# Encoder block on one core: row-maximum scores in 64-row matmuls, two key blocks at a time, with 1024-column maxima

## The chip, the core and the metric

One Trainium2 chip, one of its cores. The metric is the time of one execution of the whole program on the device, in microseconds (us); lower is better. The engines are TensorE (PE in the profile, its weight loads shown apart as PEld), VectorE (DVE), ScalarE (ACT), GpSimd (POOL) and SyncE (SP), which here only issues transfers.

## What is computed

One layer of a bidirectional encoder in float32 with 2048 tokens, width 1024, 8 query heads of 64 columns that share 2 key/value heads, four pooling groups and a gated MLP of width 2816. Cut to what the change touches:

```python
h = rmsnorm(x, norm1_g[l]) * (1.0 + sc1) + sh1
proj = h @ w_in[l]                       # q | k | v | pool channels
q = apply_axial_rope(rmsnorm(q, q_norm_g[l]), tables)
k = apply_axial_rope(rmsnorm(k, k_norm_g[l]), tables)
s = jnp.einsum('bqkgd,bskd->bkgqs', qblk, k).astype(jnp.float32)   # q already times 1/8
p = jax.nn.softmax(s, axis=-1)
o = jnp.einsum('bkgqs,bskd->bqkgd', p, v)
mix = jnp.concatenate([att, pool], axis=-1) @ w_out[l]
x = x + g1 * mix                          # then the gated MLP, also added to x
```

## The kernel before

The program has three stages. The first projects the tokens into q, k, v and pool channels and writes q and k, transposed, to scratch in DRAM. The second is attention with the output projection. The third is the gated MLP. Only the second is touched, but for one copy in the first that lays k out for it.

Every float32 value that goes through TensorE is kept as two parts of a faster type, a high part (hi) and the rest (lo). A q tile `qa` has hi in partitions 0 to 63 and lo in 64 to 127; a key tile `kA` has hi in both halves. One matmul over 128 rows therefore gives (q_hi + q_lo) k_hi. A second matmul over 65 rows adds q_hi k_lo and, with a row of ones in `kB` at partition 64, minus the row maximum, which stands in partition 64 of `qb`.

Attention runs over 32 units, each one head and 512 queries (`gen_unit`). A unit goes over 16 key tiles of 128 keys. For each: two matmuls into `S` (L731, L732), two exponentials on ScalarE (L735 into `ph`, L736 in place), one subtraction on VectorE (L737 into `pl`), a running sum on GpSimd (L741) and two matmuls with v (L723 into `A`, L724 into `B`).

The row maxima of unit u+1 are worked out while unit u runs (`gen_max`, called as `nxt`): for each of four query tiles and four blocks of 512 keys, one matmul over 128 rows into one of two PSUM banks `pmx` (L692) and one VectorE reduction over 512 columns into `mx` (L694). Then `nm` is the negated maximum (L697), four small matmuls turn it into a row (L701), and ScalarE copies the row into `qb` (L702). Unit 0 has 12 of its 16 blocks done in the first stage.

A third stream, the filler, spreads the output projection of earlier chunks (L820, with L842 on VectorE) and the second norm's transposes (L860) over the units. The last chunk's output projection starts in PSUM banks that attention leaves (`gen_tail_pool`).

The order on each engine is set by a scheduler from the order of writing and the buffers; each engine then runs its instructions in that order and waits on semaphores. Loads of q go through the queue of SP from unit 3 on, of the first units through that of POOL.

Of the kernel before, what the change touches and what calls it, by code (L numbers as in the profile page):

```python
# [18 lines left out]
P = 128  # L19
# [4 lines left out]
HD = 64  # L24
# [23 lines left out]
class InOrder:  # L48
    """An engine whose instructions stay in the order in which they are written."""

# [14 lines left out]
def hybrid_block(ctx: ExitStack, tc: tile.TileContext, x, c, w_ada, b_ada, norm1_g, w_in,  # L65
# [14 lines left out]

# [1 line left out]
    q_scr = tc.dram_tile([NH, P, T], F32, name="q_scr")  # L82
# [9 lines left out]

# [1 line left out]
    const = ctx.enter_context(tc.tile_pool(name="const", bufs=1))  # L94
# [28 lines left out]

    # =============== mixer input projection ===============
    with tc.tile_pool(name="p1", bufs=1) as p1, \
            tc.tile_pool(name="ps1", bufs=1, space=PSUM) as ps1:
        # columns of w_in: q, k, v first (their space is free first), then u
        wi_hi, wi_lo = ([p1.tile([P, KD, n], F32R, name=f"wi_{nm}{n}") for n in (768, 512)]
# [171 lines left out]

        # scale and shift of the first norm; the first tokens' norm beside them
        h0 = gen_h(0)
# [16 lines left out]

        # weights, split, in the order of use  # L320
        bufs_w = [stage(), stage(), small("qst", [P, NH, P], F32), small("qhl", [P, NH, 2, HD]),
# [17 lines left out]

        # 1/count at the clipped edges  # L340
        edge = p1.tile([P, NG, 16], F32, name="edge")
# [68 lines left out]
        def gen_rope(b, tok, raw, cs_t, res):  # L410
# [25 lines left out]
            for i in range(2):  # L436
                S.copy(out=khl[:, :, i], in_=raw[:, 8:10])
            V.tensor_tensor(out=khl[:, :, 2], in0=raw[:, 8:10], in1=khl[:, :, 0].bitcast(F32),
                            op=ALU.subtract)
            S.copy(out=khl[:, :, 3], in_=ones.rearrange("p (a d) -> p a d", a=2))  # L440
            yield
# [7 lines left out]
        def gen_tr(tok, qhl, khl):  # L449
            """q as (hi, lo), k as (hi, hi) and (lo, one), transposed"""  # L450
            for _ in range(4):
                yield
            tr = ps1.tile([P, 4, P], F32R, tag="tr", name=f"trk{tok}", bufs=1)
            for a in range(NKV):
                for i in range(2):
                    PE.transpose(out=tr[:, 2 * i + a],
                                 in_=khl[:, a, 2 * i:2 * i + 2].rearrange("p a d -> p (a d)"),
                                 identity=identr)
                    yield
            kst = p1.tile([P, 2 * NKV, P], F32, tag="kst", name=f"kst{tok}", bufs=1)  # L460
            S.copy(out=kst, in_=tr.bitcast(F32))
            SP.dma_start(out=k_scr[:, :, :, tok:tok + P].rearrange("i a p t -> p (i a) t"), in_=kst)
            if tok >= T - BT:
                qst = stage().rearrange("p (h t) -> p h t", t=P)
            else:
                qst = p1.tile([P, NH, P], F32, tag="qst", name=f"qst{tok}", bufs=1)
            for hb in range(2):
                tr = ps1.tile([P, 4, P], F32R, tag="tr", name=f"tr{tok}_{hb}", bufs=1)
                for h in range(4):
                    PE.transpose(out=tr[:, h], in_=qhl[:, hb * 4 + h].rearrange("p a d -> p (a d)"),  # L470
                                 identity=identr)
                    yield
                S.copy(out=qst[:, hb * 4:hb * 4 + 4], in_=tr.bitcast(F32))
            SP.dma_start(out=q_scr[:, :, tok:tok + P].rearrange("h p t -> p h t"), in_=qst)

        def windows(b, us, res):
            """column i is token t0 - 8 + i, at column 8 + i of u; the last block has 8 more"""
            last = b == NB - 1
# [73 lines left out]
        def gen_early_max():  # L552
            """the row maxima of the first unit over the keys of the blocks that are done"""
            k0 = p1.tile([P, KD, BT], F32R, tag="h_hi", name="k_early", bufs=2).rearrange("p k t -> p (k t)")
# [73 lines left out]

    # =============== attention and output projection ===============
    ctx3 = ctx.enter_context(ExitStack())  # L630
    with tc.tile_pool(name="po", bufs=1, side="right", reuse_waits="tile") as po, \
# [7 lines left out]
        kB = p2.tile([P, NKV, T], F32R, name="kB")  # L639
        # per key tile: [v_lo 0 | v_hi 0 | ones | v_hi 1 | v_lo 1]  # L640
        vt = p2.tile([P, NKT, 5 * HD], F32R, name="vt")
# [13 lines left out]
        def load_kv(a, parts=((0, T - BT), (T - BT, T))):  # L655
            for t0, t1 in parts:
                for i, (m, n) in enumerate(((kA, P), (kB, 65))):
                    ld(a, m[0:n, a, t0:t1], k_scr[i, a, 0:n, t0:t1])
                ld(a, vt[:, t0 // P:t1 // P, 192 * a:192 * a + P],
                   v_scr[t0:t1, a].rearrange("(n p) d -> p n d", p=P))  # L660
# [9 lines left out]
        NU = len(units)  # L670
        qtiles = {}

        def load_q(u):
# [6 lines left out]
            (G if u < QG else QE).dma_start(out=qa.bitcast(F32), in_=q_scr[h, :, cs])  # L680
            (G if u < QG else QE).dma_start(out=qb[0:64].bitcast(F32), in_=q_scr[h, 0:64, cs])
            qtiles[u] = (qa, qb)

        def gen_max(u):
            c_, h = units[u]
            a = h // 4
            qa, qb = qtiles[u]
            mx = p2.tile([P, 4, 4], F32, tag="mx", name=f"mx{u}", bufs=2) if u else mx0
            for jq in range(0 if u else 4 * JP, 16):
                for j, qt in ((jq // 4, jq % 4) if u == 0 else (jq % 4, jq // 4),):  # L690
                    ps = ps2.tile([P, 512], F32, tag="mx", name=f"pmx{u}_{qt}_{j}", bufs=2)
                    PE.matmul(ps, qa[:, qt * P:(qt + 1) * P], kA[:, a, j * 512:(j + 1) * 512],  # L692
                              start=True, stop=True)
                    V.tensor_reduce(out=mx[:, qt, j:j + 1], in_=ps, axis=AX.X, op=ALU.max)  # L694
                    yield
            nm = p2.tile([P, 4], F32R, tag="nm", name=f"nm{u}", bufs=2)
            V.tensor_reduce(out=nm, in_=mx, axis=AX.X, op=ALU.max, negate=True)  # L697
            row = ps2.tile([P, 512], F32, tag="mx", name=f"row{u}", bufs=2)
            yield
            for qt in range(4):  # L700
                PE.matmul(row[0:1, qt * P:(qt + 1) * P], nm[:, qt:qt + 1], identr, start=True, stop=True)  # L701
            S.copy(out=qb[64:65, :], in_=row[0:1, :])  # L702
            yield
# [7 lines left out]
        def gen_unit(u):  # L711
# [16 lines left out]
            for kt in range(NKT):  # L728
                ks = slice(kt * P, (kt + 1) * P)
                s = ps2.tile([P, 512], F32, tag="S", name=f"S{u}_{kt}", bufs=3)  # L730
                PE.matmul(s, kA[:, a, ks], qa, start=True, stop=False)  # L731
                PE.matmul(s, kB[0:65, a, ks], qb[0:65], start=False, stop=True)  # L732
                ph = p2.tile([P, QC], F32R, tag="ph", name=f"ph{u}_{kt}", bufs=4)
# [92 lines left out]
        def gen_out(c_, half, wait=0):  # L826
            """x1 = x + pool half, then x1 += attention half."""
            if half == 1:
# [16 lines left out]
        def gen_ln2(t, x1, junk, hts, bank, stat, wait):  # L845
            """normalised x1, transposed"""
            tok = t * P
# [29 lines left out]
        LW = (4, 4)  # L877
        # the last chunk's output projection: the pool half first, in banks that the attention leaves
        tails = []

        def gen_tail_pool(tags, mix):
            for tag, bufs in tags:
                t, n = divmod(len(tails), 2)
                ps = ps2.tile([P, 512], F32, tag=tag, name=f"pt{t}_{n}", bufs=bufs)
                tails.append(ps)
                yield from gen_half(ps, mix, 1, t, n, True, False)

        mix3 = []

        def gen_first():  # L890
            mix3.extend(load_mix(NC - 1))
            for _ in range(12):
                yield
            yield from gen_tail_pool((("misc", 1), ("mx", 2), ("mx", 2)), mix3)

# [49 lines left out]

        # =============== gated conv MLP: Winograd's form of Strassen's product ===============
        pa = ctx3.enter_context(tc.tile_pool(name="pa", bufs=1, reuse_waits="tile"))
# [11 lines left out]
        def gen_ops(p, res):  # L959
            """the moving operands of part p, split"""  # L960
            o0, no, N = PARTS[p]
# [53 lines left out]
        def gen_w(p, j, res):  # L1015
            """the stationary operands of one pair of column tiles, split, in the order of use"""
            raw = []
# [82 lines left out]
    with tc.tile_pool(name="p3", bufs=1, reuse_waits="tile") as p3, \  # L1100
# [5 lines left out]
        def gen_wd(p, j, n, tag=""):  # L1106
            """w_down times the gate, split: worked out with the first part, kept in DRAM for the others"""
            rs, ns = slice(j * P, (j + 1) * P), slice(n * 512, (n + 1) * 512)
# [83 lines left out]
        def gen_gate(p, j, ug, uv):  # L1192
            """the depthwise convolution, the gate and its split"""
            o0, no, N = PARTS[p]
# [45 lines left out]
        def residual(p, i):  # L1240
            """half a tile of x1, to be added to the sum so far"""
            t, n = divmod(i, 2)
# [168 lines left out]
```

## Time and profile before

| | us |
|---|---|
| median of 3 runs | 2740.19 |
| lowest and highest run | 2736.31, 2745.56 |
| span of the profiled execution, first to last instruction | 2741.8 |
| of it, attention, from the first row maximum to the last unit | 380 to 1240 |
| TensorE, VectorE, ScalarE, GpSimd busy over the span | 2594.1, 2370.5, 1475.5, 1767.0 |

The page gives busy time as the union of the records of an engine. Matmul records overlap, since each is longer than the distance to the next one; so TensorE is better read from the starts of its matmuls than from its busy share.

### The profile page before, as it was taken

What the parts mean: (1) busy time and instruction counts of PE and PEld (TensorE: products, weight loads), DVE (VectorE), ACT (ScalarE), POOL (GpSimd) and SP (SyncE); (2) the same over time, 40 slices, a digit from 0 to 9 for tenths busy, and PEclk for the clock granted to TensorE, in tenths of its full rate; (3) what the DMA queues carried; (4) which work ended last, traced back from release to release, by engine and by line L of the source; (5) the groups of instructions that cost most, each with busy time, mean ns of one, the idle gap of its engine ahead of it and who ended that gap; (6) DMA issues with size and microseconds to landing.
All of it is one profiled execution on the core that took longest, in us unless ns stands there. A gap on an engine that the chain in (4) does not pass through costs nothing.

```text
span 2741.8 us, 39488 instructions
## 1 busy us (share of the span) xinstructions
PE 2594.1 (95%) x13439; PEld 2242.1 (82%) x13439; DVE 2370.5 (86%) x3526; ACT 1475.5 (54%) x2656; POOL 1767.0 (64%) x1397
## 2 busy tenths in 40 slices
PE   5899989999999999999899999899999998999999
PEld 5788867777776767767888888789999997999998
DVE  7778688989999998887999999978888888898886
ACT  5566457777778777775533443543333334533342
POOL 1222146556657666565888888697777776988883
PEclk9899989999999999999999999999999999999999
DMA  9685374331221222225444444443333224433332
GB/s 291 232 258 179 99 239 149 106 95 60 64 80 55 71 72 76 80 64 179 151 130 133 128 130 123 145 132 105 100 104 100 93 87 132 147 123 120 106 110 93
DMA packets 318164, 338.65 MB, mean 124 GB/s; under 512 B 24655, under 2 KB 226329, under 8 KB 317961
## 3 DMA queue, kind: packets, MB, share of 16 engines
q1 hardware_dynamic: 316953, 332.31, 38.4%
q0 software_dynamic: 1008, 3.81, 0.5%
q8 instruction: 106, 1.74, 0.3%
q14 instruction: 97, 0.79, 0.1%
HBM read 249.42 MB, written 86.63 MB: 123 GB/s over the span
## 4 chain that ended last, share of the span: by engine, by line
PE 36%; DVE 13%; issue 3%; ACT 1%; POOL 1%; POOLq 0%; DVEq 0%; ACTq 0%
PE pp L1156 23%; PE py L1233 13%; DVE y L1238 3%; DVE ac L1202 2%; DVE ac L1205 2%; DVE b L993 1%; DVE t L993 1%; ACT ac L1199 1%; PE pl L1354 1%; DVE wds L56 0%; DVE wdl L1123 0%; DVE ac L1212 0%; DVE ug L1176 0%; DVE uv L1171 0%; DVE uv L1174 0%
## 5 line engine op out<-in xcount | busy, mean ns | idle before, releaser
L1035 POOL TENSOR_TENSOR wl_s<-s,wh_s 128x512 fp32r<-128x512 f32 x260 | 390.3, 1502 | 187.8 <-ACT wh_s L1033 186.6
L1238 DVE TENSOR_TENSOR y<-py,y 128x512 f32<-128x512 f32 x620 | 418.5, 682 | 95.5 <-PE py L1233 94.8
L741 POOL TENSOR_TENSOR acc<-acc,ph 128x512 f32<-128x512 f32 x352 | 463.4, 1316 | 41.0 <-ACT ph L735 15.7
L1156 PE MATMUL pp<-t,wh_s 128*128 128x322 f32 (+1 forms) x1584 | 390.2, 322 | 7.0 <-DVE x L1072 3.2
L737 DVE TENSOR_TENSOR pl<-S,ph 128x512 fp32r<-128x512 f32 x512 | 348.7, 684 | 38.5 <-ACT S L736 31.5
L735 ACT ACTIVATE ph<-S 128x512 fp32r<-128x512 f32 x512 | 307.3, 600 | 131.9 <-PE S L732 116.2
L694 DVE TENSOR_REDUCE mx<-pmx 128x1 f32<-128x512 f32 x500 | 338.1, 681 | 27.0 <-PE pmx L692 25.2
L1035 POOL TENSOR_TENSOR wl_a<-wr,wh_a 128x512 fp32r<-128x512 f32 x195 | 312.9, 1605 | 22.7 <-ACT wh_a L1033 22.6
L1233 PE MATMUL py<-wdh,gh 128*128 128x512 f32 x674 | 275.7, 409 | 47.1 <-DVE y L1238 40.6
L736 ACT ACTIVATE S<-S 128x512 f32<-128x512 f32 x512 | 306.4, 598 | 0.0
L1156 PEld LDWEIGHTS pp<-t,wh_s 128*128 128x128 f32 x1584 | 282.2, 190 | 27.8 <-DVE t L993 4.1
L1033 ACT CAST wh_s<-s 128x512 fp32r<-128x512 f32 x264 | 161.9, 617 | 226.8 <-PE pp L1156 197.0
L1156 PE MATMUL pp<-b,wh_a 128*128 128x322 f32 (+1 forms) x1056 | 267.9, 323 | 1.3 <-DVE b L993 0.8
L1233 PE MATMUL py<-wdh,gl 128*128 128x512 f32 x674 | 268.8, 399 | 0.0
L1233 PE MATMUL py<-wdl,gh 128*128 128x512 f32 x674 | 268.8, 399 | 0.0
L1156 PE MATMUL pp<-t,wl_s 128*128 128x322 f32 (+1 forms) x792 | 254.3, 321 | 0.0
L724 PE MATMUL B<-pl,vt 128*128 128x512 f32 x512 | 210.5, 411 | 6.2 <-DVE pl L737 6.0
L1033 ACT CAST wh_a<-wr 128x512 fp32r<-128x512 f32 x198 | 122.3, 618 | 165.6 <-PE pp L1156 158.4
L723 PE MATMUL A<-ph,vt 128*128 128x512 f32 x512 | 204.7, 408 | 5.2 <-ACT ph L735 5.2
L692 PE MATMUL pmx<-kA,qa 128*128 128x512 f32 x500 | 203.3, 408 | 3.9 <-DMA kA<-k_scr 3.0
L739 POOL TENSOR_TENSOR acc<-ph,ph 128x512 f32<-128x512 f32 x32 | 41.3, 1290 | 256.8 <-ACT ph L735 226.9
L732 PE MATMUL S<-qb,kB 65*128 65x512 f32 x512 | 202.8, 402 | 1.1 <-ACT qb L702 0.8
(273 smaller groups left out, 6784.4 us busy)
## 6 DMA issues: line engine op xcount, KB each, us to landing
wr<-in_w_up_dram SPq DMA_DIRECT2D x132, 512.0 KB
wdh<-wd_scr SPq DMA_DIRECT2D x88, 256.0 KB
wdl<-wd_scr SPq DMA_DIRECT2D x88, 256.0 KB
stage<-in_w_ada_dram SPq DMA_DIRECT2D x36, 512.0 KB
x_scr<-x SPq DMA_DIRECT2D x48, 256.0 KB
wds<-in_w_down_dram SPq DMA_DIRECT2D x44, 256.0 KB
wd_scr<-wdh SPq DMA_DIRECT2D x44, 256.0 KB
wd_scr<-wdl SPq DMA_DIRECT2D x44, 256.0 KB
```

Of the source, the lines that this page charges most:

```text
L694: V.tensor_reduce(out=mx[:, qt, j:j + 1], in_=ps, axis=AX.X, op=ALU.max)
L723: PE.matmul(A, vt[:, kt, 192 * a:192 * a + P], ph, start=kt == 0, stop=kt == NKT - 1)
L724: PE.matmul(B, vt[:, kt, 64 + 64 * a:192 + 64 * a], pl, start=kt == 0, stop=False)
L735: S.activation(out=ph, in_=s, func=AF.Exp, scale=0.125)
L736: S.activation(out=s, in_=s, func=AF.Exp, scale=0.125)
L737: V.tensor_tensor(out=pl, in0=s, in1=ph.bitcast(F32), op=ALU.subtract)
L741: G.tensor_tensor(out=acc, in0=acc, in1=ph.bitcast(F32), op=ALU.add)
L1033: S.copy(out=hf, in_=src)
L1035: eng.tensor_tensor(out=lf, in0=src, in1=hf.bitcast(F32), op=ALU.subtract)
L1156: mm = PE.matmul(ps, l_[:, k], r_[:, k, 0:N], start=k == 0 and m == 0, stop=k == 3 and m == 2)
L1233: PE.matmul(ps, l_[:, ts_], r_, start=i == 0, stop=i == 3 * len(js) - 1)
L1238: V.tensor_tensor(out=ys[t][:, ns], in0=ps, in1=ys[t][:, ns], op=ALU.add)
```

## The change

Each maximum is now taken over q_hi k_hi alone. A pair of key blocks is scored by two matmuls over 64 rows, one on partitions 0 to 63 (`qa`, key block 2jj) and one on partitions 64 to 127 (`qb`, key block 2jj+1), into the two banks of one PSUM tile. One VectorE reduction then takes the maximum over 1024 columns. To have q_hi in both places, `qb` is loaded twice, and the row of minus maxima moves to its partition 0; `kB` therefore has (one and zeros) in its upper half and lo in its lower, and the second matmul of `S` goes over 128 rows. The buffer ring of two single banks becomes one tile of two banks.

```diff
-            V.tensor_tensor(out=khl[:, :, 2], in0=raw[:, 8:10], in1=khl[:, :, 0].bitcast(F32),
+            V.tensor_tensor(out=khl[:, :, 3], in0=raw[:, 8:10], in1=khl[:, :, 0].bitcast(F32),
                             op=ALU.subtract)
-            S.copy(out=khl[:, :, 3], in_=ones.rearrange("p (a d) -> p a d", a=2))
+            S.copy(out=khl[:, :, 2], in_=onesz[:, 127:191].unsqueeze(1).broadcast_to([P, NKV, HD]))
...
-                for i, (m, n) in enumerate(((kA, P), (kB, 65))):
-                    ld(a, m[0:n, a, t0:t1], k_scr[i, a, 0:n, t0:t1])
+                for i, m in enumerate((kA, kB)):
+                    ld(a, m[:, a, t0:t1], k_scr[i, a, :, t0:t1])
...
-            (G if u < QG else QE).dma_start(out=qb[0:64].bitcast(F32), in_=q_scr[h, 0:64, cs])
+            for r in (0, 64):
+                (G if u < QG else QE).dma_start(out=qb[r:r + 64].bitcast(F32), in_=q_scr[h, 0:64, cs])
...
-            mx = p2.tile([P, 4, 4], F32, tag="mx", name=f"mx{u}", bufs=2) if u else mx0
-            for jq in range(0 if u else 4 * JP, 16):
-                for j, qt in ((jq // 4, jq % 4) if u == 0 else (jq % 4, jq // 4),):
-                    ps = ps2.tile([P, 512], F32, tag="mx", name=f"pmx{u}_{qt}_{j}", bufs=2)
-                    PE.matmul(ps, qa[:, qt * P:(qt + 1) * P], kA[:, a, j * 512:(j + 1) * 512],
-                              start=True, stop=True)
-                    V.tensor_reduce(out=mx[:, qt, j:j + 1], in_=ps, axis=AX.X, op=ALU.max)
-                    yield
+            def pair(nm):
+                return ps2.tile([P, 2, 512], F32, tag="mx", name=f"{nm}{u}", bufs=1)
...
+                mx = p2.tile([P, 4, 2], F32, tag="mx", name=f"mx{u}", bufs=2)
+                for qt in range(4):
+                    qs = slice(qt * P, (qt + 1) * P)
+                    for jj in range(2):
+                        ps = pair(f"pmx{qt}_{jj}_")
+                        for t, q_ in ((0, qa), (1, qb)):
+                            r, j = slice(64 * t, 64 * t + 64), 2 * jj + t
+                            PE.matmul(ps[:, t], q_[r, qs], kA[r, a, j * 512:(j + 1) * 512],
+                                      start=True, stop=True)
+                        yield
+                        V.tensor_reduce(out=mx[:, qt, jj:jj + 1], in_=ps.rearrange("p a n -> p (a n)"),
+                                        axis=AX.X, op=ALU.max)
+                        yield
...
-            row = ps2.tile([P, 512], F32, tag="mx", name=f"row{u}", bufs=2)
+            row = pair("row")[:, 0]
...
-            S.copy(out=qb[64:65, :], in_=row[0:1, :])
+            S.copy(out=qb[0:1, :], in_=row[0:1, :])
+            maxed.append(u)
...
-                PE.matmul(s, kB[0:65, a, ks], qb[0:65], start=False, stop=True)
+                PE.matmul(s, kB[:, a, ks], qb, start=False, stop=True)
```

Unit 0 keeps single 512-column maxima, and the tail's pool half takes both banks of the pair at once, after the last maxima are done.

On TensorE, in the third unit (its score tiles are `S`, the row maxima of the fourth unit are `pmx`), before:

```order
L731 MATMUL S_4_4928<-qa_4259,kA 128x512
L732 MATMUL S_4_4928<-qb_4260,kB 128x512
L723 MATMUL A_4858<-ph_2_4895,vt 128x512
L724 MATMUL B_4859<-pl_2_4896,vt 128x512
L692 MATMUL pmx_1_0_4939<-kA,qa_4538 128x512
L731 MATMUL S_5_4944<-qa_4259,kA 128x512
L732 MATMUL S_5_4944<-qb_4260,kB 128x512
L723 MATMUL A_4858<-ph_3_4910,vt 128x512
L724 MATMUL B_4859<-pl_3_4911,vt 128x512
L692 MATMUL pmx_1_1_4955<-kA,qa_4538 128x512
```

and at the same key tiles now:

```order
L754 MATMUL S_4_4896<-qa_4261,kA 128x512
L755 MATMUL S_4_4896<-qb_4262,kB 128x512
L746 MATMUL A_4829<-ph_2_4865,vt 128x512
L747 MATMUL B_4830<-pl_2_4866,vt 128x512
L754 MATMUL S_5_4912<-qa_4261,kA 128x512
L755 MATMUL S_5_4912<-qb_4262,kB 128x512
L712 MATMUL pmx_0_3_4907<-kA,qa_4523 128x512
L712 MATMUL pmx_0_3_4907<-kA,qb_4524 128x512
L746 MATMUL A_4829<-ph_3_4880,vt 128x512
L747 MATMUL B_4830<-pl_3_4881,vt 128x512
```

A single `pmx` matmul per key tile has become two neighbours per two key tiles. There are 248 such pairs; in 237 the two stand next to each other, in 11 one full matmul stands between them. From the end of one pair to the start of the next there are mostly 7 to 13 other matmuls.

On VectorE, at the same place, before:

```order
L737 TENSOR_TENSOR pl_4_4932<-S_4_4928,ph_4_4931 128x512
L694 TENSOR_REDUCE mx_4868<-pmx_1_0_4939 128x1
L737 TENSOR_TENSOR pl_5_4948<-S_5_4944,ph_5_4947 128x512
L694 TENSOR_REDUCE mx_4868<-pmx_1_1_4955 128x1
L694 TENSOR_REDUCE mx_4868<-pmx_1_2_4970 128x1
L737 TENSOR_TENSOR pl_6_4963<-S_6_4959,ph_6_4962 128x512
```

and now:

```order
L760 TENSOR_TENSOR pl_4_4900<-S_4_4896,ph_4_4899 128x512
L760 TENSOR_TENSOR pl_5_4916<-S_5_4912,ph_5_4915 128x512
L715 TENSOR_REDUCE mx_4839<-pmx_0_3_4907 128x1
L760 TENSOR_TENSOR pl_6_4929<-S_6_4925,ph_6_4928 128x512
L715 TENSOR_REDUCE mx_4839<-pmx_1_3_4936 128x1
```

Sixteen reductions per unit have become eight of twice the columns, each between one or two subtractions.

## Rows read from the trace of the kernel before

**Rows 1.** The page: the span, and each engine's busy us (share of it) xinstructions.

```profile
span 2741.8 us, 39488 instructions
...
PE 2594.1 (95%) x13439; PEld 2242.1 (82%) x13439; DVE 2370.5 (86%) x3526; ACT 1475.5 (54%) x2656; POOL 1767.0 (64%) x1397
```

**Rows 2.** Windows over attention: length, then each engine's busy us (instructions), granted clock, DMA.

```profile
380.00:600.00 220.00, 212.84 (x895) 163.70 (x895) 192.36 (x316) 155.55 (x287) 128.65 (x99) 0.97 0.45 146
600.00:800.00 200.00, 198.37 (x855) 153.68 (x854) 182.04 (x300) 147.46 (x275) 121.47 (x94) 1.00 0.21 65
800.00:1240.00 440.00, 421.60 (x1797) 312.47 (x1796) 396.84 (x646) 345.96 (x654) 282.03 (x234) 0.99 0.25 73
```

**Rows 3.** The same windows, matmuls of L692 (the row-maximum scores) alone.

```profile
380.00:600.00 220.00, 54.45 (x130) 25.66 (x130) 0.97 0.45 146
600.00:800.00 200.00, 47.55 (x120) 22.61 (x120) 1.00 0.21 65
800.00:1240.00 440.00, 101.25 (x251) 47.60 (x250) 0.99 0.25 73
```

**Rows 4.** Groups on VectorE, 600 to 800 us: busy us, mean ns | idle before, releaser.

```profile
L694 DVE TENSOR_REDUCE mx<-pmx 128x1 f32<-128x512 f32 x119 | 80.7, 681 | 5.1 <-PE pmx L692 4.7
...
L697 DVE TENSOR_REDUCE nm<-mx 128x4 fp32r<-128x16 f32 x8 | 1.3, 164 | 0.0
```

**Rows 5.** Line L860: ns min/median/max, first and last start, form.

```profile
L860 PE MATMUL tp<-ident,lx x96: 270/272/421, 806.1 to 1186.2; 128*128 128x128 f32 x96
```

**Rows 6.** Timeline of PE in attention: start us, length us, line, tiles, rows*columns of the array.

```profile
702.53 0.40 PE L732 MATMUL S<-qb,kB 65*128 65x512 f32 x1
...
704.86 0.40 PE L692 MATMUL pmx<-kA,qa 128*128 128x512 f32 x1
```

**Rows 7.** Timeline of DVE over the same stretch.

```profile
701.37 0.67 DVE L694 TENSOR_REDUCE mx<-pmx 128x1 f32<-128x512 f32 x1
...
702.57 0.67 DVE L694 TENSOR_REDUCE mx<-pmx 128x1 f32<-128x512 f32 x1
```

**Rows 8.** Waits from 600 to 800 us: total us, times, longest us.

```profile
PEld B L724 <- DVE pl L737: 4.1, 10, 1.1
...
PEld pmx L692 <- DVE mx L694: 0.8, 3, 0.3
```

**Rows 9.** Timeline of PE where full-height matmuls alternate with one-row ones.

```profile
236.10 1.12 PE L242 MATMUL mr<-macc,ones 128*128 128x512 f32 x2 [0.78 <-DVE macc L200]
237.16 1.12 PE L243 MATMUL mr<-stage,ones 1*128 1x512 f32 x2
...
240.31 0.39 PE L374 MATMUL pu<-h_hi,wi_hi 128*128 128x256 f32 x1
240.54 0.28 PE L374 MATMUL pu<-h_lo,wi_hi 128*128 128x256 f32 x1
240.66 0.29 PE L374 MATMUL pu<-h_hi,wi_lo 128*128 128x256 f32 x1
```

**Rows 10.** The same place, a narrower window: the second matmul of the first block alone.

```profile
236.63 0.59 PE L242 MATMUL mr<-macc,ones 128*128 128x512 f32 x1
```

**Rows 11.** The same place, a weight load (PEld) after the last one-row block.

```profile
240.31 0.19 PEld L374 LDWEIGHTS pu<-h_hi,wi_hi 128*128 128x128 f32 x1 [0.76 <-DVE win L490]
```

**Rows 12.** Timeline of PE around the one-column matmuls of a unit's end.

```profile
893.34 0.40 PE L758 MATMUL B<-al,onesr 128*128 128x512 f32 x1
893.57 0.40 PE L701 MATMUL row<-identr,nm 128*1 128x128 f32 x4
893.81 0.45 PE L692 MATMUL pmx<-kA,qa 128*128 128x512 f32 x1
894.10 0.64 PE L820 MATMUL po<-wo,atth 128*128 128x512 f32 x2
```

**Rows 13.** VectorE on 1024 columns, line L200: ns min/median/max, first and last start.

```profile
L200 DVE SCALAR_TENSOR_TENSOR macc<-stage,cact,macc x30: 1275/1281/1286, 24.9 to 234.8; 128x1024 f32<-128x1024 f32 x30
```

**Rows 14.** POOL's queue just before attention: the load that its first matmul waits for.

```profile
376.63 0.57 POOL L653 DMA_DIRECT2D kA<-k_scr x1 [3.11 <-DMA k_scr<-kst]
```

More of the change, by code (lines that the diff above doesn't have):

```diff
@@ L670, in hybrid_block @@
         NU = len(units)
-        qtiles = {}
+        qtiles, maxed = {}, []
         def load_q(u):
@@ L687, in gen_max @@
             qa, qb = qtiles[u]
-            mx = p2.tile([P, 4, 4], F32, tag="mx", name=f"mx{u}", bufs=2) if u else mx0
-            for jq in range(0 if u else 4 * JP, 16):
-                for j, qt in ((jq // 4, jq % 4) if u == 0 else (jq % 4, jq // 4),):
-                    ps = ps2.tile([P, 512], F32, tag="mx", name=f"pmx{u}_{qt}_{j}", bufs=2)
-                    PE.matmul(ps, qa[:, qt * P:(qt + 1) * P], kA[:, a, j * 512:(j + 1) * 512],
-                              start=True, stop=True)
-                    V.tensor_reduce(out=mx[:, qt, j:j + 1], in_=ps, axis=AX.X, op=ALU.max)
-                    yield
+            def pair(nm):
+                return ps2.tile([P, 2, 512], F32, tag="mx", name=f"{nm}{u}", bufs=1)
+            if u == 0:
+                mx = mx0
+                for i in range(2):
+                    ps = pair(f"pmx{i}_")
+                    for t in range(2):
+                        qt = 2 * i + t
+                        PE.matmul(ps[:, t], qa[:, qt * P:(qt + 1) * P], kA[:, a, JP * 512:(JP + 1) * 512],
+                                  start=True, stop=True)
+                        V.tensor_reduce(out=mx[:, qt, JP:JP + 1], in_=ps[:, t], axis=AX.X, op=ALU.max)
+                        yield
+            else:
+                mx = p2.tile([P, 4, 2], F32, tag="mx", name=f"mx{u}", bufs=2)
[6 more added lines that the diff above has]
+                            PE.matmul(ps[:, t], q_[r, qs], kA[r, a, j * 512:(j + 1) * 512],
+                                      start=True, stop=True)
+                        yield
+                        V.tensor_reduce(out=mx[:, qt, jj:jj + 1], in_=ps.rearrange("p a n -> p (a n)"),
+                                        axis=AX.X, op=ALU.max)
+                        yield
             nm = p2.tile([P, 4], F32R, tag="nm", name=f"nm{u}", bufs=2)
             V.tensor_reduce(out=nm, in_=mx, axis=AX.X, op=ALU.max, negate=True)
-            row = ps2.tile([P, 512], F32, tag="mx", name=f"row{u}", bufs=2)
+            row = pair("row")[:, 0]
             yield
@@ L882, in gen_tail_pool @@
             for tag, bufs in tags:
+                while tag == "mx" and NU - 1 not in maxed:
+                    yield
                 t, n = divmod(len(tails), 2)
-                ps = ps2.tile([P, 512], F32, tag=tag, name=f"pt{t}_{n}", bufs=bufs)
-                tails.append(ps)
-                yield from gen_half(ps, mix, 1, t, n, True, False)
+                if tag == "mx":
+                    ps = ps2.tile([P, 2, 512], F32, tag=tag, name=f"pt{t}_{n}", bufs=bufs)
+                    two = [ps[:, 0], ps[:, 1]]
+                else:
+                    two = [ps2.tile([P, 512], F32, tag=tag, name=f"pt{t}_{n}", bufs=bufs)]
+                for ps in two:
+                    t, n = divmod(len(tails), 2)
+                    tails.append(ps)
+                    yield from gen_half(ps, mix, 1, t, n, True, False)
         mix3 = []
@@ L893, in gen_first @@
                 yield
-            yield from gen_tail_pool((("misc", 1), ("mx", 2), ("mx", 2)), mix3)
+            yield from gen_tail_pool((("misc", 1), ("mx", 1)), mix3)
         load_q(0)
```

## The prediction

> **What bounds the kernel now.** The page comes first: TensorE is busy 95% of the span and VectorE 86% [rows 1]. Those shares mix stages, and the change acts in attention alone, so the next view is the windows over attention [rows 2]. They hold 860 of the 2741.8 us. VectorE is busy 182 of 200 us in the middle window and 396.84 of 440 in the last, so both engines are candidates there.
>
> A busy TensorE says little, because a matmul's record is longer than its turn. The timeline gives the turn: from the matmul at 702.53 to that at 704.86 there are 10 steps, so one 512-column matmul takes 0.233 us when nothing is late [rows 6]. With that I work out what TensorE needs in each window. The other forms are few: four one-column matmuls for every 16 row-maximum scores, four in 0.24 us [rows 12], and 96 transposes after 806 us [rows 5]. A transpose's record is 0.27 us, a 512-column one's is 0.39 for a turn of 0.23, so 0.16 is tail and a transpose's turn about 0.11.
> - 600 to 800: 855 matmuls, 30 of them one-column (120/16*4, [rows 3]): 825*0.233 + 1.8 = 194.0 us. Idle: 6.0 us, 3.1% of the needed time.
> - 380 to 600: 895, 32 one-column: 203.0 of 220 us, 17.0 idle. The start of attention lies in it.
> - 800 to 1240: 1797, 63 one-column, 96 transposes: 1638*0.233 + 3.8 + 10.6 = 396.1 of 440, idle 43.9, 10%.
>
> So in the first two windows TensorE sets the time, nearly alone; in the last it waits for a tenth of the time for others. The waits from 600 to 800 agree: TensorE's weight loads wait only 4.1 us in all for `pl` and 0.8 us for a free maximum bank [rows 8]. The granted clock is 0.97 to 1.00 [rows 2], the 2.4 GHz level.
>
> **The change part by part.**
>
> *The maximum on VectorE.* 496 reductions of 512 columns become 248 of 1024. Now, from 701.37 to 702.57, two instructions take 1.20 us, so one turn is 0.60 [rows 7]. For 1024 columns there is no reduction. The two reductions in the trace take 164 ns for 16 columns and 681 for 512, that is 1.04 ns a column [rows 4]; 512 more columns then add 0.53 us to a turn of 0.60, 1.13 in all. The only 1024-column rows, of another operation on SBUF, take 1.28 us [rows 13], longer than two turns. I take 1.13, because the operation and the source are the same, and keep 1.20, no gain, as the other end. Saved: 248*(1.20 - 1.13) = 17 us of VectorE, or 0.
>
> *The scores on TensorE.* This decides. The number of matmuls does not fall; two 64-row ones could run side by side in the array. If they do, they take one turn, 0.23 us in place of 0.465. But 64-row matmuls now stand singly between full-height ones, as the order shows: two in, then 7 to 13 of the others. The trace has no 64-row matmul. Its nearest rows are one-row matmuls between full-height ones [rows 9]. There a block of two takes 237.16 - 236.10 = 1.06 us, and three blocks 240.31 - 237.16 = 3.15. The second matmul of a block has a record of 0.59 us [rows 10], less the tail of 0.16 a turn of 0.43. Its block's successor could start at 236.63 + 0.43 = 237.06 and starts at 237.16: 0.10 us late. And the first matmul after a change takes 0.23 us to its successor where the next takes 0.12 [rows 9]: its weight load was not done ahead. The PEld row says the same, as the load at 240.31 starts with its matmul after 0.76 us of idle [rows 11]. That is 0.11 us more. A change of height so costs about 0.21 us, each way; two blocks of 0.86 plus 0.21 give the 1.07 that the rows show as 1.06.
>
> A pair between full-height matmuls then takes 0.10 + 0.11 to get in, 0.23 side by side, 0.10 + 0.11 to get out: 0.65. If the second tile's weights are loaded after the first's, 0.11 more: 0.76. Against 0.465 now that is 0.19 or 0.30 more. I take the middle, 0.25, as nothing in the trace separates them. If the two do not run side by side, it is 0.465 + 0.42 = 0.885, 0.42 more. The other bound is the change to one-column matmuls [rows 12]: the first of them starts 0.23 us after its predecessor, no delay, and only the first after them costs 0.29 in place of 0.23. By that a pair is 0.23 + 0.06 = 0.29, 0.175 less than now. I choose the one-row rows over the one-column rows because the change here is in the height of the contraction too.
>
> The Trainium skill, "TensorEngine Tiling (Array Packing)", section Key Properties, states that a change of tiling mode drains TensorE. The trace agrees where the height changes (0.10 us late) and does not where only the columns do. The sum by that rule would be the one chosen here.
>
> So the pairs add 248*0.25 = 62 us of TensorE turns, between 47 and 74, or 104 if serial. In 11 pairs a full matmul stands between the two; each pays a second change in and out (0.42) and loses the side-by-side turn, about 0.6 us, 7 in all.
>
> *The single pair buffer.* Two banks that turned over one by one become one that turns over in twos. A pair's successor waits for the reduction: 1.13 us, up to 0.60 for a subtraction ahead of it in VectorE's order. That is 1.7 us, while 7 to 13 other matmuls take 1.6 to 3.0. Mostly free; where pairs stand closer TensorE waits some tenths. Behind a late pair stand the next `A` and `S` matmuls, and ScalarE waits for `S`. I put it at nothing and let the rival below carry it.
>
> *The rest.* The second matmul of `S` over 128 rows in place of 65 costs nothing: a 65-row matmul's record is as long as a full-height one's, 0.40 us both [rows 6]. One more load of 128 KB per unit goes into DMA engines that are 21 to 45% busy [rows 2], three units ahead of use. Of the extra issues on POOL's queue, two stand ahead of the last `kA` load, at about 0.57 us each; that load's issue sat 3.11 us waiting for `k_scr` [rows 14], which covers 1.1 us. Without that cover it would be 1 us. The copies of k in the first stage only change place.
>
> *The sum.* TensorE's needed time grows in each window by its pairs. I add 3.1% of idle, which is what the fullest window has now, and keep the 10.7 us by which the first window exceeds that (start of attention).
> - 380 to 600: 63 pairs, 203.0 + 15.8 + 2 = 220.8; times 1.031, plus 10.7: 238.3, +18.3.
> - 600 to 800: 60 pairs, 194.0 + 15 + 2 = 211.0; times 1.031: 217.5, +17.5.
> - 800 to 1240: 125 pairs, 396.1 + 31.3 + 3 = 430.4; times 1.031: 443.7, +3.7. Most of the extra fits into the idle tenth.
>
> Together +40. Against it stands VectorE's saving in the first two windows, 123*0.07 = 8.6 us, which shortens some of the waits that remain; I take half, 4. The profile would then be 2741.8 + 36 = 2778. The median of the runs lies 1.6 below this profile: **2776**, 1.3% slower.
>
> **The rivals.**
> - *Cheap change of height, faster.* If 64-row pairs behave like the one-column matmuls, a pair saves 0.175 us. Then the windows need 11, 10.5 and 22 us less TensorE. The first two fall by 11 each; in the last TensorE is not the bound, and only VectorE's 125*0.07 = 9 can come off. That is -31: 2709. For it: rows 12 show a mode without delay. Against: the one-row rows, four changes with the same price. It decides against me as soon as the change there and back costs less than the 0.23 that the side-by-side turn saves. The Trainium skill, "TensorE: Matmul & The Clock Gate", Part 3, Measured speedup vs the span model, gives packed row tiles the span of one matmul plus about 4 ns for each further tile; no row here shows it, and taken without a cost of change it leads to this rival.
> - *No cover, slower still.* If idle time stays as it is, because VectorE's 1.13 us reductions hold up `pl` and the single buffer holds up pairs, the whole 69 us come through: 2809. If in addition the two tiles run one after the other, the three windows by the same formula give +29, +28 and +26: 2823. For it: reductions twice as long between subtractions, and waits on `pl` exist already [rows 8]. Against: 0.8 us of waits for a bank.
> - *All absorbed, no change.* At 0.19 a pair, TensorE's extra is 54 us, and today's idle time in attention is 66.9. If it is all filled, and VectorE's 17 us shorten the rest, the time stays within 8 us of 2740. Against: 600 to 800 has only 6.0 us to give for 60 pairs.
>
> **How the numbers follow.** My forecast gets 0.44 (its own range 2760 to 2792: 0.19 a pair with all of VectorE's 8.6 us, or 0.30 with none), no cover 0.18, all absorbed 0.14, cheap change 0.24. A measurement here tells from no change what exceeds 0.3%, 8 us. Faster is the cheap change, 0.24; same is the absorbed case, 0.14; slower is the other two, 0.62. The range leaves out half of the cheap case, below its 2709, and a third of the no-cover case, above 2815: 2709 to 2815.
>
> **What would show it.** Right: in the timeline of the changed kernel the first matmul of a pair starts about 0.33 us after its predecessor, and the one after the pair has its weight load not ahead; from the start of the matmul ahead of a pair to that of the second full one after it there is about 0.25 us more than four turns. Attention grows from 860 to about 896 us, most of it before 800 us, and the last window hardly. VectorE's reductions have records near 1.21 us. The chain of waits shows TensorE's own time, not `mx`. Wrong: pairs spaced like ordinary turns with the second matmul starting at nearly the same time as the first, or new waits of tens of us on `mx`, or a longer first window because the first loads land later.

## The result and the profile after

| | before | after |
|---|---|---|
| median | 2739.31 us (2736.31 to 2745.56, 4 runs) | 2789.2 us (2787.16 to 2792.12, 4 runs) |
| profiled span | 2741.8 us | 2787.7 us |

The changed kernel takes 1.0178 times as long (95% interval 1.0162 to 1.0193), 50 us more. The forecast was 2776 in a range of 2709 to 2815; the direction was right, the size 13 us short.

The page of the changed kernel, to be read against [rows 1]; behind `|` stand busy us, mean ns, then idle us before and its releaser:

```profile
span 2787.7 us, 39455 instructions
...
PE 2633.2 (94%) x13439; PEld 2189.3 (79%) x13439; DVE 2356.4 (85%) x3278; ACT 1474.3 (53%) x2655; POOL 1771.8 (64%) x1400
...
L760 DVE TENSOR_TENSOR pl<-S,ph 128x512 fp32r<-128x512 f32 x512 | 347.1, 686 | 69.5 <-ACT S L759 64.5
L758 ACT ACTIVATE ph<-S 128x512 fp32r<-128x512 f32 x512 | 305.9, 597 | 178.9 <-PE S L755 169.8
L715 DVE TENSOR_REDUCE mx<-pmx 128x1 f32<-128x1024 f32 x248 | 301.9, 1217 | 32.7 <-PE pmx L712 32.0
```

The subtraction and the first exponential before:

```profile
L737 DVE TENSOR_TENSOR pl<-S,ph 128x512 fp32r<-128x512 f32 x512 | 348.7, 684 | 38.5 <-ACT S L736 31.5
L735 ACT ACTIVATE ph<-S 128x512 fp32r<-128x512 f32 x512 | 307.3, 600 | 131.9 <-PE S L732 116.2
```

VectorE lost 14 us of busy time, and both VectorE and ScalarE now stand idle longer (69.5 us after 38.5, and 178.9 after 131.9) ahead of the work that hangs on the scores `S`. What is late is TensorE. The windows over attention, as in [rows 2], show how much less it gets done:

```profile
380.00:600.00 220.00, 207.37 (x813) 137.33 (x814) 169.14 (x229) 138.90 (x258) 116.67 (x93) 0.93 0.45 146
600.00:800.00 200.00, 199.09 (x822) 134.46 (x820) 174.98 (x234) 143.48 (x268) 119.47 (x93) 1.00 0.26 76
800.00:1240.00 440.00, 421.08 (x1730) 276.23 (x1730) 379.16 (x504) 330.57 (x625) 267.99 (x219) 0.99 0.26 75
```

Its busy time is nearly what it was, its count fell from 895, 855 and 1797 to 813, 822 and 1730. Each matmul takes more of the time. Which ones, the timeline of TensorE around one pair shows (start us, length us, line, tiles, rows*columns of the array):

```profile
702.97 0.39 PE L747 MATMUL B<-pl,vt 128*128 128x512 f32 x1
703.29 0.50 PE L712 MATMUL pmx<-kA,qa 64*128 64x512 f32 x1
703.29 0.49 PE L712 MATMUL pmx<-kA,qb 64*128 64x512 f32 x1
703.72 0.50 PE L754 MATMUL S<-qa,kA 128*128 128x512 f32 x1
704.05 0.40 PE L755 MATMUL S<-qb,kB 128*128 128x512 f32 x1
704.29 0.40 PE L746 MATMUL A<-ph,vt 128*128 128x512 f32 x1
```

and the weight loads of the same place:

```profile
703.29 0.18 PEld L712 LDWEIGHTS pmx<-kA,qa 64*128 64x128 f32 x1 [0.36 <-issue]
703.29 0.18 PEld L712 LDWEIGHTS pmx<-kA,qb 64*128 64x128 f32 x1
703.72 0.19 PEld L754 LDWEIGHTS S<-qa,kA 128*128 128x128 f32 x1 [0.24 <-issue]
703.82 0.19 PEld L755 LDWEIGHTS S<-qb,kB 128*128 128x128 f32 x1
```

The two 64-row matmuls do run side by side. But the pair starts 0.32 us after its predecessor instead of 0.233, the full matmul behind it waits 0.43, and the one after that 0.33. Over the 237 pairs that stand undivided the medians are 0.326, 0.003, 0.428 and 0.339 us, together 1.095 against four turns of 0.932: **0.16 us more a pair**. The loads show where most of it goes: neither the pair's weights nor those of the first full matmul behind it are loaded ahead, as in [rows 11].

The start of attention is longer too. POOL's queue and TensorE there (`x2` in the first row are the two loads of `qb` that the change makes of one):

```profile
376.19 1.05 POOL L682 DMA_DIRECT2D qb<-q_scr  x2
383.29 0.57 POOL L653 DMA_DIRECT2D kA<-k_scr  x1 [6.04 <-issue]
```

```profile
388.93 0.79 PE L699 MATMUL pmx<-kA,qa 128*128 128x512 f32 x1 [6.47 <-DMA kA<-k_scr]
390.51 0.80 PE L699 MATMUL pmx<-kA,qa 128*128 128x512 f32 x1 [0.78 <-DVE mx L701]
...
395.45 0.59 PE L723 MATMUL row<-identr,nm 128*1 128x128 f32 x4 [0.99 <-DVE nm L719]
396.70 0.80 PE L755 MATMUL S<-qb,kB 128*128 128x512 f32 x1 [0.66 <-ACT qb L724]
```

The last `kA` load is issued at 383.29 where it was at 376.63 [rows 14]; the idle ahead of it is now put down to `issue`, not to the store. Unit 0's four maxima go through one pair buffer, so each matmul waits 0.78 us for the reduction before it; from the first of them to the row of maxima it is 6.52 us. The second matmul of the first `S` starts at 396.70 us; before the change it starts at 387.43 us, 9.3 earlier. Not all of the 9.3 us is the change. The last store of k to scratch is issued at 374.73 us here and at 371.46 before, and in the traces of later runs, whose first stage is that of the changed kernel, between 366.0 and 375.9. Counted from this store the first unit starts after 22.0 us in place of 16.0: 6.0 us more, 3.4 of them up to the issue of the load and 2.6 from the first maximum to the row.

### The profile page after: what moved, and what is told of

It reads as the page before. It is cut to its first block, busy times and chain, and to the rows that moved or that the text cites. A ratio compares the mean times of both kernels' runs of the same rounds, so it can differ in the third digit from the quotient of the medians.

```text
span 2787.7 us, 39455 instructions
## 1 busy us (share of the span) xinstructions
PE 2633.2 (94%) x13439; PEld 2189.3 (79%) x13439; DVE 2356.4 (85%) x3278; ACT 1474.3 (53%) x2655; POOL 1771.8 (64%) x1400
## 4 chain that ended last, share of the span: by engine, by line
PE 34%; DVE 14%; issue 3%; ACT 1%; POOL 1%; DMA 0%; DVEq 0%; POOLq 0%; ACTq 0%
PE pp L1187 21%; PE py L1264 12%; DVE y L1269 3%; DVE ac L1233 2%; DVE ac L1236 2%; DVE b L1024 1%; ACT ac L1230 1%; DVE wdl L1154 1%; PE pl L1385 1%; DVE t L1024 1%; DVE wds L56 1%; DVE gl L1252 1%; DVE ac L1243 0%; DVE ug L1207 0%; DVE uv L1205 0%
## 5 line engine op out<-in xcount | busy, mean ns | idle before, releaser
L760 DVE TENSOR_TENSOR pl<-S,ph 128x512 fp32r<-128x512 f32 x512 | 347.1, 686 | 69.5 <-ACT S L759 64.5
L758 ACT ACTIVATE ph<-S 128x512 fp32r<-128x512 f32 x512 | 305.9, 597 | 178.9 <-PE S L755 169.8
L715 DVE TENSOR_REDUCE mx<-pmx 128x1 f32<-128x1024 f32 x248 | 301.9, 1217 | 32.7 <-PE pmx L712 32.0
L746 PE MATMUL A<-ph,vt 128*128 128x512 f32 x512 | 212.2, 424 | 9.5 <-ACT ph L758 6.9
L755 PE MATMUL S<-qb,kB 128*128 128x512 f32 x512 | 205.5, 405 | 4.5 <-ACT qb L724 4.4
L754 PE MATMUL S<-qa,kA 128*128 128x512 f32 x512 | 205.4, 406 | 0.0
```

Source lines behind the costliest of these rows:

```text
L715: V.tensor_reduce(out=mx[:, qt, jj:jj + 1], in_=ps.rearrange("p a n -> p (a n)"), axis=AX.X, op=ALU.max)
L746: PE.matmul(A, vt[:, kt, 192 * a:192 * a + P], ph, start=kt == 0, stop=kt == NKT - 1)
L758: S.activation(out=ph, in_=s, func=AF.Exp, scale=0.125)
L760: V.tensor_tensor(out=pl, in0=s, in1=ph.bitcast(F32), op=ALU.subtract)
```

## The experiments

After the trace two theories stood. A: the cost is TensorE's, paid at each pair for the change of height, with some 10 us at the start. B: it is VectorE's and the pair buffer's, because a reduction of 1.2 us holds up what is queued behind it. Each run's ratio is to runs of the kernel before on the same chip (medians 2740.1 to 2741.0); in brackets stands its 95% interval, and 0.001 of it is 2.7 us.

### full_height: the pair over 128 rows

```diff
-                            PE.matmul(ps[:, t], q_[r, qs], kA[r, a, j * 512:(j + 1) * 512],
+                            PE.matmul(ps[:, t], qa[:, qs], kA[:, a, j * 512:(j + 1) * 512],
```

> The two matmuls of a pair go over all 128 rows (qa against kA, both key blocks), as before the change; the pair's two-bank tile, the single buffer, the 1024-column reduction and the start stay. So TensorE never changes height for the scores. Theory A (the changes of height are the cost): the changed kernel's trace has 0.32 us into a pair, 0.003 between its two matmuls, 0.43 out of it and 0.34 after, 1.09 us where four turns take 0.93; without the changes 248 * 0.16 = 39 us go, 2789 becomes about 2750. Rival B (the single buffer and the 1024-column reductions hold TensorE up): nothing of that changes, and TensorE has 248 turns more to do, 2789 or more.

2750.2 us, ratio 1.0035 (1.0022 to 1.0048). With the reduction, the buffer and the start of the changed kernel, but full-height matmuls, 39 us of the 50 are gone. A holds for these; B cannot be more than the remainder.

### half_the_pairs: 64 rows for two of four query tiles

```diff
                             r, j = slice(64 * t, 64 * t + 64), 2 * jj + t
+                            if qt >= 2:
+                                q_, r = qa, slice(0, P)
                             PE.matmul(ps[:, t], q_[r, qs], kA[r, a, j * 512:(j + 1) * 512],
```

> 64-row pairs for the first two query tiles of each unit, full-height ones for the other two; all else as in the changed kernel. Theory A: half of the changes of height, so half of the 39 us come off, about 2770, midway between the changed kernel and the one with none. Rival B: no trend, 2789 as the changed kernel.

2768.97 us, ratio 1.0099 (1.0082 to 1.0116): 18.8 us above full_height, half of 39. The price goes by the number of pairs, 0.15 us each. The traces say the same without the start: from the second matmul of the first `S` to the last row of reciprocals (`rb_last`) attention takes 860.2 us with no 64-row pair, 878.7 with half of them and 896.4 with all; before the change it takes 858.5.

### two_reductions: 64-row pairs, two reductions of 512 columns

```diff
-                        V.tensor_reduce(out=mx[:, qt, jj:jj + 1], in_=ps.rearrange("p a n -> p (a n)"),
-                                        axis=AX.X, op=ALU.max)
+                        for t in range(2):
+                            V.tensor_reduce(out=mx[:, qt, 2 * jj + t:2 * jj + t + 1], in_=ps[:, t],
+                                            axis=AX.X, op=ALU.max)
```

> 64-row pairs as in the changed kernel, but each bank has its own 512-column reduction, so VectorE has 496 of about 0.60 us again and none of 1.13. Theory A: TensorE's changes of height are unmoved; VectorE gets 248 * 0.07 = 17 us more work, part of which shows: 2789 to 2800. Rival B: if the long reductions held up the subtractions ahead of B's matmuls, shorter ones give time back: under 2780.

2795.08 us, ratio 1.0198 (1.0178 to 1.0218). Without the long reduction it is no faster; the interval overlaps that of the changed kernel. B falls as the cause of the 50 us; what the one pair buffer costs this run doesn't show, since it keeps it.

### start_as_before: the first loads and unit 0's maxima

```diff
+        def load_q_rest(u):
+            c_, h = units[u]
+            cs = slice(c_ * QC, (c_ + 1) * QC)
+            G.dma_start(out=qtiles[u][1][64:128].bitcast(F32), in_=q_scr[h, 0:64, cs])
...
         load_kv(0, ((T - BT, T),))
+        load_q_rest(0)
         load_q(2)
+        load_q_rest(1)
+        load_q_rest(2)
```

(The loads taken out of `load_q` for the first three units stand behind the last key and value loads in POOL's queue, and unit 0's maxima alternate between the pair buffer and the bank `misc`.)

> Only the start of attention: the second loads of qb for the first three units are issued behind the last loads of k and v, and unit 0's four maxima take turns in two separate tiles. The changed kernel's last kA load is issued 8.6 us after k_scr's store where it was 5.2 before (3.4 us), and its four maxima take 6.5 us from first score to row where they took 4.0 (2.6 us). If both lie on the path: 2789 - 6 = 2783. If the rest of attention swallows them: 2789.

2778.56 us, ratio 1.0143 (1.0122 to 1.0164): 10.6 us less than the changed kernel, with runs from 2773 to 2784, where 6 were expected. POOL and TensorE in its trace:

```profile
375.25 0.57 POOL L653 DMA_DIRECT2D kA<-k_scr  x1 [4.05 <-DMA k_scr<-kst]
```

```profile
380.56 0.80 PE L705 MATMUL pmx<-kA,qa 128*128 128x512 f32 x1 [3.31 <-DMA kA<-k_scr]
...
385.77 0.79 PE L761 MATMUL S<-qb,kB 128*128 128x512 f32 x1 [0.67 <-ACT qb L730]
```

The load waits for the store again, as in [rows 14], and the first unit starts at 385.77 instead of 396.70; counted from the last store of k, after 16.6 us instead of 22.0. The two edits were made together; what each is worth was not tried.

### full_height_start: both together

> Each pair's two matmuls take all 128 rows (qa against kA, 465 ns a pair instead of two that run together), as in full_height, and the start is as in start_as_before. What is left of the change is the one 1024-column reduction for a pair. If the two parts add up, 2750.2 less the 10.6 us that the start was worth: 2740, no different from before (2741), and the 1024-column reduction is worth nothing although it takes 17 us of VectorE's time away. Rival: those 17 us are worth their length once the start no longer hides them, 2724 to 2730.

2741.43 us, ratio 1.0007 (0.9995 to 1.0019). What is left of the change, one 1024-column reduction for a pair out of one buffer, is worth nothing. The start gives 8.8 us here and 10.6 with 64 rows, and the 64 rows cost 37 us with this start and 39 with the other: within the spread of the runs the two parts add up.

### full_two_reductions: full height, two reductions

Its reductions are those of two_reductions, its matmuls those of full_height.

> As full_height (both matmuls of a pair over 128 rows, changed start, one pair buffer), but with two reductions of 512 columns for a pair in place of one of 1024. It puts VectorE's 17 us back (248 times 0.07) and nothing else. If VectorE's time is off the path: 2750 to 2754. If it is on the path: 2767.

2773.6 us, ratio 1.0126 (1.0108 to 1.0145), 23 us above full_height and above both bounds. So with one pair buffer the one reduction is worth 23 us against two, more than the 17 us of VectorE's time that it saves, and something else in the pairs takes as much. The idle time of the weight loads and matmuls of `B` (us, times) in this kernel,

```profile
  DVE pl L761: 26.8, 48
```

and in full_height:

```profile
  DVE pl L760: 11.3, 36
```

That is 15.5 us more, in waits for VectorE's subtraction.

### full_one_a_step and before_two_a_step: what takes VectorE's time back

The first hands out full_two_reductions' reductions one a turn. The second is the kernel before, with its two separate banks, but two scores in one turn and their two reductions in the next.

```diff
+                        two = [score(qt, 2 * jj + t) for t in range(2)]
+                        yield
+                        for t in range(2):
+                            reduce(qt, 2 * jj + t, two[t])
+                        yield
```

> full_two_reductions with its two 512-column reductions in two turns, one in each, in place of both in the second turn; VectorE does the same work with the same one pair buffer. If the 23 us between full_two_reductions and full_height come from two reductions that stand in a row and hold up the low parts of the exponentials (L761) behind them: 2752 to 2760. If they come from VectorE's time itself or from the pair buffer that is freed as a whole: 2770 to 2775.

> The kernel before (two separate one-bank buffers, four 512-column reductions a tile, its own start) with one edit: two score matmuls are handed out in one turn and their two reductions together in the next, which gives VectorE the order of full_two_reductions (two low parts, two reductions). If that order on VectorE is what made full_two_reductions 22 us slower than the kernel before (beyond the start's 10.6): 2758 to 2764. If it is the one buffer for a pair, which comes free as a whole: 2738 to 2746.

2770.13 us, ratio 1.0112 (1.0096 to 1.0128), and 2748.83 us, ratio 1.0033 (1.0023 to 1.0042). The turn of a reduction is not it. Two scores and two reductions at a time cost 9 us in the kernel before. Of the 33 us between that kernel and full_two_reductions, 9 to 11 are the start and 9 this order; some 14 are left, and no run shows what they are. The one buffer, freed as a whole, is a candidate, but TensorE hardly waits for it. The waits from 800 to 1240 us (total us, times, longest us), first in before_two_a_step, then in full_two_reductions:

```profile
PEld pmx L691 <- DVE mx L696: 5.0, 19, 0.5
```

```profile
PEld pmx L712 <- DVE mx L716: 0.2, 1, 0.2
PEld A L747 <- ACT ph L759: 41.5, 117, 1.9
```

What grew is the wait of `A` for `ph`, which is 25.6 us in before_two_a_step. The order of the instructions, which the scheduler makes from the buffers, and the loads and rows of the changed kernel differ between the two as well.

### full_start_apart: the two full-height scores a turn apart

```diff
+                            if t == 0:
+                                yield
-                        yield
```

> full_height_start (2741) with the two full-height matmuls of a pair in two turns, one in each as before the change, and the 1024-column reduction in the second turn. If what eats VectorE's 17 us is that two score matmuls come in a row on TensorE, it is faster than both: 2725 to 2733. If it is that a reduction now takes 1.13 us in one piece, or that VectorE's time was not on the path, it stays at 2738 to 2743.

2753.4 us, ratio 1.005 (1.0034 to 1.0067), 12 us more than with the two together. It was expected to stay or to gain. By the trace the pair buffer is held a little longer, from the first score's start to the reduction's end 2.70 us on average in place of 2.49, and TensorE's weight loads wait 18.0 us for `mx` in place of 12.2. That is half of the 12 us at most; the rest stays open.

### pair_twice: each pair's matmuls issued twice

```diff
-                        for t, q_ in ((0, qa), (1, qb)):
+                        for t, q_ in ((0, qa), (1, qb), (0, qa), (1, qb)):
```

> The changed kernel with each pair's two matmuls issued a second time into the same two banks, so that the same scores are worked out twice. If the price is paid on entering and leaving the 64-row rows, and two of them go side by side, the second two add one pitch of 0.233 us: 248 times 0.233 is 58 us, and some 29 more pieces of groups that other matmuls split, at about 0.2 us, 6 us: 2853. Rival: two 64-row matmuls do not really go side by side and add two pitches, 0.465: 2911. Second rival: each 64-row matmul pays for itself (0.39 each): 2789 + 193 = 2982.

2855.05 us, ratio 1.042 (1.0398 to 1.0442), 2 us from the sum. A group of four on TensorE:

```profile
650.26 0.40 PE L747 MATMUL B<-pl,vt 128*128 128x512 f32 x1
650.59 0.49 PE L712 MATMUL pmx<-kA,qa 64*128 64x512 f32 x1
650.59 0.49 PE L712 MATMUL pmx<-kA,qb 64*128 64x512 f32 x1
650.92 0.39 PE L712 MATMUL pmx<-kA,qa 64*128 64x512 f32 x1
650.93 0.39 PE L712 MATMUL pmx<-kA,qb 64*128 64x512 f32 x1
651.25 0.51 PE L843 MATMUL po<-wo,mix 128*128 128x512 f32 x1
651.59 0.39 PE L754 MATMUL S<-qa,kA 128*128 128x512 f32 x1
```

The way in and out is paid once, and the second two are nearly free of it. Medians over 208 such groups: 1.322 us from the matmul ahead to the second full one behind, where six full turns take 1.398. By this spacing four 64-row matmuls together are 0.08 us cheaper than four full ones; two are 0.16 dearer. Four at once need four maximum banks, twice what there is, so no kernel was made of it.

### split_pairs and split_same_steps: pairs pulled apart

split_pairs adds a turn between the two 64-row matmuls; split_same_steps moves the second one into the turn of the reduction.

```diff
                             PE.matmul(ps[:, t], q_[r, qs], kA[r, a, j * 512:(j + 1) * 512],
                                       start=True, stop=True)
+                            if t == 0:
+                                yield
```

(split_same_steps also drops the `yield` behind the loop.)

> The changed kernel with the two 64-row matmuls of a pair handed out in two turns, so that other matmuls fall between them: in the order on TensorE 75 pairs are split instead of 11. A 64-row matmul that stands alone between full ones should cost 0.326 + 0.428 + 0.339 less three full pitches of 0.233, which is 0.39 us, twice a pair is 0.79, against 0.16 for a pair whose two go side by side: 64 times 0.62 is 40 us, 2829. Rival: the cost goes by the number of 64-row matmuls, not by how often the height changes, and a pair costs the same split or not: 2789.

> The changed kernel with the second 64-row matmul of a pair handed out one turn later, together with the reduction, so that a unit's maxima take the same sixteen turns as in the changed kernel (split_pairs took 24 and could not finish inside the unit). In the order on TensorE 92 pairs are split by other matmuls instead of 11. By the records of the split kernel a lone 64-row matmul costs 0.328 + 0.428 + 0.341 less three pitches of 0.233, 0.40 us, so a split pair 0.80 against 0.16: 81 times 0.64 is 52 us, 2841. If the rest of split_pairs' 117 us came from the split itself and not from the turns, it comes out near 2900.

2906.47 us, ratio 1.0609 (1.0588 to 1.0629), and 2835.79 us, ratio 1.0344 (1.0324 to 1.0364). The first missed by 77 us, the second by 5. A lone 64-row matmul in split_same_steps:

```profile
682.74 0.40 PE L755 MATMUL S<-qa,kA 128*128 128x512 f32 x1
683.08 0.49 PE L712 MATMUL pmx<-kA,qa 64*128 64x512 f32 x1
683.50 0.50 PE L756 MATMUL S<-qb,kB 128*128 128x512 f32 x1
683.84 0.40 PE L747 MATMUL A<-ph,vt 128*128 128x512 f32 x1
```

The spacing is that of a whole pair, and 81 more split pairs cost 47 us, 0.57 each. What split_pairs pays beyond that is its turns: with 24 for a unit's maxima they are not done inside the unit before. The copy of the row into `qb` then waits, in split_pairs

```profile
  PE row L725: 137.7, 31
```

and in split_same_steps

```profile
  PE row L724: 44.9, 21
```

And the granted clock falls in split_pairs (us, TensorE busy, clock, DMA):

```profile
900.00:1000.00 100.00, 89.76 (x330) 0.91 0.19 52
```

In split_same_steps it is 1.00 there.

## Why the prediction was right in direction and short in size

- *The price of a pair: mechanism right, size too high.* I had seen two matmuls side by side, with a late start and unhidden weight loads on both sides, and left open whether the second tile's weights load after the first's: 0.19 or 0.30, taken 0.25. Both loads start together at 703.29, so the upper price is out. Measured: the pair starts 0.09 us late, the first matmul behind it 0.20 and the second 0.11, less the 0.23 that the side-by-side turn saves: 0.16. The term was 62 + 7 = 69 us; by the records it is 237 times 0.16 plus 11 times 0.80, 47, and full_height gives 39. The Trainium skill, "TensorEngine Tiling (Array Packing)", Key Properties, states that a change of tiling mode drains TensorE; the 0.09 us agree with it, though no run shows that a drain is what they are. The Trainium skill, "TensorE: Matmul & The Clock Gate", Part 3, Measured speedup vs the span model, gives about 4 ns for each further tile; the 3 ns between the two matmuls agree, and that model has no cost for the change.
- *The idle tenth of the last window: wrong.* "Most of the extra fits into the idle tenth" gave +3.7 for the last window, after +18.3 and +17.5. From the starts of units 0, 8 and 16 and of the last row of reciprocals, in us, attention grew by 11.7, 9.5 and 16.6. Before and after:

```profile
606.79 0.50 PE L732 MATMUL S<-qb,kB 65*128 65x512 f32 x1
...
819.08 0.48 PE L732 MATMUL S<-qb,kB 65*128 65x512 f32 x1
...
L787 PE MATMUL rb_last<-o,ones x2: 588/625/662, 1245.5 to 1246.0; 1*128 1x512 f32 x2
```

```profile
627.76 0.49 PE L755 MATMUL S<-qb,kB 128*128 128x512 f32 x1
...
849.55 0.49 PE L755 MATMUL S<-qb,kB 128*128 128x512 f32 x1 [0.90 <-ACT qb L724]
...
L810 PE MATMUL rb_last<-o,ones x2: 587/624/662, 1292.6 to 1293.1; 1*128 1x512 f32 x2
```

  The differences are 21.0, 30.5 and 47.1 us, after the 9.3 of the first unit. For 64, 64 and 120 pairs that is 0.18, 0.15 and 0.14 us each: the last window paid for its pairs nearly like the others, and its idle time, which comes from waits between engines, took up little of the extra work. In the sum the too high price and this step cancelled, which is luck: without the first unit's 9.3 us attention grew by 37.8, and the forecast had 36.
- *"Covers 1.1 us. Without that cover it would be 1 us": wrong.* The two extra issues ahead of the last `kA` load moved it by more than their own 1.1 us, and unit 0's four maxima through one buffer, 2.6 us longer, had no term at all. By the trace these are 6.0 us, by the runs 9 to 11, with intervals of 5 to 7 us each way. That is most of what the forecast lacked; the rest lies within that spread. A longer first window was among the prediction's own signs of being wrong, and it came.
- *The reduction at 1.13 us: right.* From 701.56, where one starts, to the next VectorE instruction is 1.17, in other places 1.13; the record has 1.217. Rows:

```profile
704.73 1.22 DVE L715 TENSOR_REDUCE mx<-pmx 128x1 f32<-128x1024 f32 x1
705.86 0.68 DVE L760 TENSOR_TENSOR pl<-S,ph 128x512 fp32r<-128x512 f32 x1
```

- *VectorE's saving at 4 us and the pair buffer at nothing: both mis-sized, sum nearly right.* At full height one reduction instead of two is worth 23 us, and taking the scores in pairs costs about as much: 9 of it, by before_two_a_step, is the order, and the rest is not explained. The net is 0.6 us. With 64-row pairs the second reduction costs only 6, which is within the spread of the runs. VectorE's longer idle time behind a slower TensorE may be the reason; that was not tried.
- *The rivals.* Cheap change of height: out, 0.16 dearer and not 0.175 cheaper. No cover: the waits for `mx` (14.4 us over 40 waits of L712's weight loads) stayed small. All absorbed: out.

Of the 50 us, 37 to 39 are the 64-row matmuls, most of the rest (9 to 11 by the runs) is the start, and the reduction with its buffer is nothing. No version beat the kernel before.

## What to carry to other kernels

Matmuls over half the rows pay on TensorE only in groups: here one pair between full-height matmuls loses 0.16 us, four in a row gain 0.08 by their spacing, and one alone loses 0.40 against one full-height matmul. Before two narrow instructions are traded for a wide one, look at what the pairing does to the order and the buffers around it: here it took back what the engine saved. And when an engine that sets the pace gets more work, count all of it, in windows with idle time too.

## What the hardware showed that was not expected

- POOL's issue of a load stood 6.04 us with nothing that the trace shows as its releaser, after two more loads had been issued ahead of it; in full_height it was 8.97 us. With those two moved behind it, the wait was for the store, 4.05 us. Why was not tried.
- After the longer wait at the start the granted clock stays at 0.50, the 1.2 GHz level, for longer: matmuls of 0.6 to 0.8 us last until 406 us, where before the change they last until 392. Part of the start's cost is this, by the windows before and in the changed kernel (us, TensorE busy, clock, DMA):

```profile
390.00:400.00 10.00, 9.95 (x36) 0.86 1.03 400
```

```profile
380.00:400.00 20.00, 9.33 (x20) 0.50 1.05 361
400.00:410.00 10.00, 9.89 (x26) 0.66 0.92 347
410.00:420.00 10.00, 9.74 (x39) 1.00 0.01 2
```

- Two weight loads into different row halves of the array run at the same time, 0.18 us each, both starting at 703.29.
